# A conformer and attention trunk in fp32: pairs of FF columns moved between two forms of the up-projection

## The chip, the core and the metric

The kernel runs on one core of one Trainium2 chip. A core has engines that run side by side: TensorE (PE; its weight loads are listed as PEld), VectorE (DVE), ScalarE (ACT), GpSimd (POOL) and SyncE (SP), which here only issues DMAs. The metric is device microseconds of one execution; lower is better. The kernel before has a median of 1044.91 us over three runs (1043.2 to 1046.06).

## The reference

512 tokens of width 1024 go through two layers, each followed by a SwiGLU FFN of 2816 columns; a final RMSNorm ends it.

```python
# layer 0: causal conformer convolution, then FFN
h = h + conformer_conv(rmsnorm(h, norm_mix[0]), ...)   # pw1, GLU, 31-tap depthwise conv, LayerNorm, silu, pw2
h = h + swiglu_ffn(rmsnorm(h, norm_ffn[0]), w_up[0], w_down[0])
# one shared k and v, then layer 1: sliding-window attention with sinks, then FFN
kv = rmsnorm(h, norm_kv) @ w_kv
q = rmsnorm(h, norm_mix[1]) @ w_q[0]
h = h + banded_sink_attention(q, k, v, sinks, rel_bias) @ w_o[0]
h = h + swiglu_ffn(rmsnorm(h, norm_ffn[1]), w_up[1], w_down[1])

def swiglu_ffn(x, w_up, w_down):
    gate, up = jnp.split(x @ w_up, 2, axis=-1)
    return (jax.nn.silu(gate) * up) @ w_down
```

All of it is float32.

## The kernel before

Channels lie on partitions, tokens along the free dimension. An fp32 product is made of three matmuls of a reduced type: high by high, high by low and low by high part (`mm3`). Every weight chunk therefore has to be split: `split_weights` casts the high part on ACT (L294) and subtracts the low part on DVE (L297).

Weights come as 258 chunks of 512 KB in an order written out by hand, `PLAN`. `advance` keeps three queues ahead of PE: SP loads nine chunks ahead into six `raw` buffers, ACT and DVE split three ahead into four `whi` and four `wlo` buffers, PE uses. Instructions of an engine run in the order in which the program issues them, so a cast that waits for a buffer holds up what stands behind it. The chunks up to pair 0 of part 0 are not split (`NATIVE`).

An FFN is worked in 11 pairs: pair p has 256 gate and 256 up columns, 4 up chunks and, later, 2 down chunks. There are three forms of the up-projection.

- By token halves (layer 0): part 0 does the first 256 tokens, part 1 the other 256. `HALVES0` gives the pairs, before 0 to 3. Part 1 uses the twin form, in which one matmul of 512 columns and one of 256 do the work of three of 256 (`mm2`, L412 and L413).
- Plain (`plain_pair`): all 512 tokens, matmuls of 512 columns. Before, only layer 1's pair 0.
- By seven products (`SevenPair`, `product`): the block product of 2 x 2 blocks by seven multiplications instead of eight (`SEVEN`), each with 24 matmuls of 256 columns. Sums S1 to S4 of weight blocks are made ahead by accumulating DMAs on POOL's queue (`prepare`, at a pace `share`) and copies on SP's; sums T1 to T4 of the rows in `Rows0.sums` (layer 0, DVE) and `Rows.sums` (layer 1, POOL at L759). A11, A12, ... name the products by their left factor; `take` gathers a product's bank into the four results c11 to c22. Before, layer 0's pairs 4 to 10 and layer 1's pairs 1 to 10.

Layer 0 runs so: the first convolution half, then part 0 (`pw2` of the first half, `ffn_part`), and beside part 0's matmuls the second half's convolution (`Half.background`: taps on DVE, ACT and POOL). `job` gives a background generator points (chunk, step), and `pace` steps it at each chunk. At its end the statistics are turned (`scales_a`, L1067 on PE), spread over the partitions by one matmul (`spread`, L1089), and the rows z are normalised, put through silu and split (`rows`: L1101, L1102, L1103, L544, L545). The products A12 of pairs 4, 5 and 6 that need only first-half rows come early, between part 0 and part 1 (`FIRST`), and ACT copies them (L1257). Part 1 starts with `pw2(h1.z, n1)`, which needs z. Then follow the products of pairs 4 to 10 with `gates` at the end of each pair, their downs, shared k and v, q and attention, o, and layer 1's FFN (`STEPS1`). Layer 1's down projections are by seven too (`low_pairs`).

Of the kernel before, what the change touches and what calls it, by code (L numbers as in the profile page):

```python
# [18 lines left out]
P = 128  # L19
# [38 lines left out]
SEVENS = tuple(range(1, FT // 2))  # L58

def by_seven(layer, pair):  # L60
    return pair in SEVENS if layer else pair >= HALVES0[1][0]


def ups(layer, pair):
    return [("up", layer, pair, half, which) for half in range(2) for which in range(2)]
# [26 lines left out]
def chunk_plan():  # L92
# [12 lines left out]
    for part in range(2):  # L105
        pw2()
        for pair in range(*HALVES0[0]):
            plan.extend(ups(0, pair))
# [15 lines left out]
    for kind, pair in STEPS1:  # L124
        plan.extend(blocks_of(kind, pair) if kind == "low" or by_seven(1, pair) else ups(1, pair))
# [84 lines left out]
def hybrid_trunk(ctx: ExitStack, tc: tile.TileContext, xT, W, prm_in, wdw_in, sinks, relb, onehot, fin, lead, out):  # L210
# [164 lines left out]

    def mm3(out, w, x, start, stop, **kw):
        if w[1] is None:
            nc.tensor.matmul(out, w[0], x, start=start, stop=stop)  # L378
            return
        nc.tensor.matmul(out, w[0], x[0], start=start, stop=False, **kw)  # L380
        nc.tensor.matmul(out, w[0], x[1], start=False, stop=False, **kw)  # L381
        nc.tensor.matmul(out, w[1], x[0], start=False, stop=stop, **kw)  # L382
# [201 lines left out]

    def ffn_part(layer, part, xg, tok, rms, on_h=None, twin=False, plain=None):
# [3 lines left out]
        for g in range(2):  # L589
# [27 lines left out]
            if w == 256:  # L617
                rs_bc = rms.step2().unsqueeze(1).to_broadcast([P, 2, w])
                for e, b in enumerate(full):
                    i = g * 4 + 2 * e  # L620
                    nc.vector.tensor_mul(b, b, rs_bc)
                    nc.vector.tensor_add(hT[:, i:i + 2, tok], b, hT[:, i:i + 2, tok])
                    for k in range(2 if on_h is not None else 0):
                        on_h(i + k)
# [110 lines left out]
    class Rows:  # L735
# [13 lines left out]
        def sums(self):  # L749
# [7 lines left out]
            for name, t, f, a, b in (("T1", t1, nc.gpsimd.tensor_sub, b11, b12), ("T2", b11, nc.gpsimd.tensor_add, b22, t1),  # L757
                                     ("T3", b12, nc.gpsimd.tensor_sub, b22, b12), ("T4", b21, nc.gpsimd.tensor_sub, b11, b21)):
                pool_op(f(t, a, b))  # L759
# [3 lines left out]
                split([both[:, e] for e in range(2)], t, name == "T2")  # L763

# [3 lines left out]
    def plain_pair(pair, rows, pool):  # L768

        banks = accs(512)  # L770
        steps = None
        for half in range(2):
            for which in range(2):
                w = get("up", 1, pair, half, which)
                order = [(k, m) for k in range(4) for m in range(2)]
                if half == 1:
                    order = [(k, m) for m in range(2) for k in range(4)]
                for k, m in order:
                    mm3(banks[which * 2 + m], [a[:, k, m * P:(m + 1) * P] for a in w], rows.x[half * 4 + k],
                        half == 0 and k == 0, half == 1 and k == 3)  # L780
                if half == 0 and which == 0:
                    rows.rms.step1()
                    continue

                if pair == 0:
                    steps = steps or rows.sums()
                    for _ in range(1 + half):
                        next(steps, None)
        rs_bc = rows.rms.step2().rearrange("p (s q) -> p s q", s=2)
        c = new_gates(pool)  # L790
        for m in range(2):
            t = temp()
            nc.vector.tensor_mul(t.rearrange("p (s q) -> p s q", s=2), banks[m].rearrange("p (s q) -> p s q", s=2), rs_bc)
            nc.scalar.activation(t, t, AF.Silu)
            nc.vector.tensor_mul(c[:, m, :, 0, :], banks[2 + m].rearrange("p (s q) -> p s q", s=2),
                                 t.rearrange("p (s q) -> p s q", s=2))
        return c
# [14 lines left out]
    class SevenPair:  # L812

        def __init__(self, kind, pair, rows, c, c11=None):
            self.kind, self.pair, self.rows, self.c, self.early = kind, pair, rows, c, c11
            self.chains = {}

        def take(self, a):
            c11, c12, c21, c22 = (self.c[:, m, s] for m in range(2) for s in range(2))
            chain = CHAINS[a][0]  # L820
# [5 lines left out]
            if a == "A11":  # L826
                if self.early is None:
                    nc.scalar.copy(c11, r)
                else:
                    nc.vector.tensor_add(c11, r, self.early)  # L830
            elif a == "S1":
                nc.scalar.mul(c22, r, -1.0)
            elif a == "S2":
# [864 lines left out]
```

## Time and profile before

The profiled execution took 1043.27 us, 1.64 below the median of the three runs; its span is 1041.5 us, and its mean TensorE clock is 0.997 of full speed.

| engine | busy us | share | instructions |
|---|---|---|---|
| PE | 1031.5 | 99% | 6580 |
| PEld | 932.6 | 90% | 6580 |
| DVE | 776.5 | 75% | 1202 |
| ACT | 613.0 | 59% | 1062 |
| POOL | 473.2 | 45% | 569 |

The span, cut at the first matmul of each stage:

| stage | from us | length us | DVE busy us |
|---|---|---|---|
| first half, pw1 of both | 0 | 128.8 | 107.37 |
| part 0: pw2 | 128.8 | 28.9 | 25.46 |
| part 0: four pairs up | 157.7 | 50.9 | 48.53 |
| part 0: downs | 208.6 | 26.1 | 19.43 |
| three early products | 234.7 | 9.1 | 9.07 |
| part 1: pw2 | 243.8 | 23.0 | 18.77 |
| part 1: ups | 266.8 | 45.9 | 37.62 |
| part 1: downs | 312.7 | 22.5 | 22.30 |
| pairs 4 to 10 by seven | 335.2 | 134.4 | 99.08 |
| their downs | 469.6 | 73.6 | 29.54 |
| kv, q, attention, o | 543.2 | 153.6 | 96.88 |
| layer 1, pair 0 (plain) | 696.8 | 23.1 | 19.66 |
| layer 1, pair 1 | 719.9 | 24.0 | 18.29 |
| layer 1, the rest | 743.9 | 279.7 | 213.25 |
| end | 1023.6 | 17.9 | 11.31 |

How to read the rows in the next sections: a timeline row has the start and the duration in us, engine, line, operation, output<-inputs, partitions x elements, and in brackets the idle time before it with what ended it ("x2": two instructions run together). A row of a wait list has engine and line that waited, the releaser, total us, times, longest us. A stage row has from:to, length, then busy us and count of PE, PEld, DVE, ACT and POOL, the granted TensorE clock, the DMA share and GB/s. A group row has line, engine, operation, shapes and count, then busy us and mean ns of one, then idle time before it. The records of matmuls overlap; their rate is read from start to start.

### The profile page before, as it was taken

Reading aid. Unit: us, or ns where it says so; the run is one execution under the profiler, and the core shown is the slowest. Engines: PE = TensorE matmul, PEld = TensorE weight load, DVE = VectorE, ACT = ScalarE, POOL = GpSimd, SP = SyncE. Lnnn points to the kernel's source line nnn. Section 1 sums busy time; section 2 is a strip of 40 time slices with the busy share of each in tenths; the row PEclk is TensorE's granted clock in tenths of the full one; section 3 lists DMA queues with packets and bytes.
Section 4 is the critical chain, followed back from the end, with each engine's and each line's share of the span. In section 5 each row is a group of like instructions: output and inputs, shape, how many; then the busy total and the mean of one; then the engine's idle time right before and its main releaser. Section 6 shows DMA issues by size and latency. Waiting matters only on the chain.

```text
span 1041.5 us, 17709 instructions
## 1 busy us (share of the span) xinstructions
PE 1031.5 (99%) x6580; PEld 932.6 (90%) x6580; DVE 776.5 (75%) x1202; ACT 613.0 (59%) x1062; POOL 473.2 (45%) x569
## 2 busy tenths in 40 slices
PE   9999999999999999999999999999999999999996
PEld 8888889999988999998888877788989999898995
DVE  3999989978789777673536566678686877868777
ACT  3887798847776556552333565466655556554654
POOL 3999999930535233221214255405442334434134
PEclk9999999999999999999999999999999999999998
DMA  9999747999999988999969766955879988877742
GB/s 356 340 315 207 205 126 204 272 256 275 249 239 262 304 220 284 256 301 244 286 209 254 210 183 183 228 154 152 252 230 312 287 264 264 245 233 222 224 150 81
DMA packets 67282, 248.33 MB, mean 238 GB/s; under 512 B 7579, under 2 KB 13884, under 8 KB 66364
## 3 DMA queue, kind: packets, MB, share of 16 engines
q1 hardware_dynamic: 54236, 200.75, 55.9%
q0 software_dynamic: 12672, 46.14, 24.8%
q8 instruction: 51, 0.84, 0.3%
q10 hardware_dynamic: 288, 0.31, 0.1%
q14 instruction: 35, 0.29, 0.1%
HBM read 241.93 MB, written 97.52 MB: 326 GB/s over the span
## 4 chain that ended last, share of the span: by engine, by line
PE 98%; DMA 0%; DVE 0%; issue 0%; POOLq 0%; SPq 0%; POOL 0%; ACT 0%
PE bank L380 20%; PE bank L382 20%; PE bank L381 20%; PE bank L960 10%; PE bank L902 9%; PE bank L412 4%; PE bank L378 4%; PE bank L413 2%; PE bank L1441 1%; PE bank L1483 1%; PE bank L1470 1%; PE bank L1058 1%; PE bank L1607 1%; PE bank L948 1%; DMA both<-in_lead_dram 0%; PE bank L1562 0%
## 5 line engine op out<-in xcount | busy, mean ns | idle before, releaser
L297 DVE TENSOR_TENSOR wlo<-raw,whi 128x1024 fp32r<-128x1024 f32 x246 | 329.7, 1348 | 136.8 <-ACT whi L294 136.5
L294 ACT CAST whi<-raw 128x1024 fp32r<-128x1024 f32 x246 | 257.1, 1049 | 276.6 <-PE bank L381 194.1
L380 PE MATMUL bank<-quad,whi 128*128 128x256 f32 (+1 forms) x976 | 307.4, 317 | 0.0
L381 PE MATMUL bank<-quad,whi 128*128 128x256 f32 (+1 forms) x976 | 306.6, 315 | 0.0
L382 PE MATMUL bank<-quad,wlo 128*128 128x256 f32 (+1 forms) x976 | 305.7, 315 | 0.0
L380 PEld LDWEIGHTS bank<-quad,whi 128*128 128x128 f32 x976 | 185.5, 191 | 12.8 <-issue 1.6
L381 PEld LDWEIGHTS bank<-quad,whi 128*128 128x128 f32 x976 | 186.0, 191 | 11.9 <-issue 0.5
L382 PEld LDWEIGHTS bank<-quad,wlo 128*128 128x128 f32 x976 | 185.6, 191 | 11.8 <-issue 0.4
L853 POOL TENSOR_TENSOR up<-up 128x512 f32<-128x512 f32 x34 | 62.9, 1851 | 283.6 <-ACT up L850 283.6
L1002 POOL TENSOR_TENSOR pr<-pr,pr 128x256 f32<-128x256 f32 x208 | 155.4, 788 | 2.6 <-ACT pr L1001 2.5
L380 PE MATMUL bank<-rows,whi 128*128 128x256 f32 x488 | 138.0, 283 | 0.0
L381 PE MATMUL bank<-rows,whi 128*128 128x256 f32 x488 | 137.8, 282 | 0.0
L382 PE MATMUL bank<-rows,wlo 128*128 128x256 f32 x488 | 137.8, 282 | 0.0
L1009 DVE SCALAR_TENSOR_TENSOR bank<-apad,wdw,bank 128x256 f32<-128x256 f32 x248 | 112.4, 485 | 3.4
L1001 ACT ACTIVATE pr<-apad,wdw 128x256 f32<-128x256 f32 x208 | 98.3, 502 | 14.9 <-POOL pr L1002 13.1
L960 PE MATMUL bank<-quad,w 128*128 128x256 f32 x448 | 98.7, 380 | 0.0
L960 PEld LDWEIGHTS bank<-quad,w 128*128 128x128 f32 x448 | 84.9, 190 | 11.8 <-DVE bank L1009 0.2
L380 PEld LDWEIGHTS bank<-rows,whi 128*128 128x128 f32 x488 | 93.1, 191 | 0.3
L381 PEld LDWEIGHTS bank<-rows,whi 128*128 128x128 f32 x488 | 93.1, 191 | 0.3
L382 PEld LDWEIGHTS bank<-rows,wlo 128*128 128x128 f32 x488 | 93.0, 191 | 0.0
L491 POOL TENSOR_TENSOR tmp<-tmp,tmp 128x256 f32<-128x256 f32 (+1 forms) x28 | 26.8, 957 | 101.4 <-ACT tmp L487 96.2
L412 PE MATMUL bank<-quad,whi 128*128 128x512 f32 x168 | 59.7, 398 | 0.0
(230 smaller groups left out, 1635.9 us busy)
## 6 DMA issues: line engine op xcount, KB each, us to landing
raw<-in_W_dram SPq DMA_DIRECT2D x170, 512.0 KB, 5.7
raw<-sum SPq DMA_DIRECT2D x88, 512.0 KB, 5.4
sum<-in_W_dram SPq DMA_DIRECT2D x52, 512.0 KB, 6.2
sum<-in_W_dram POOLq DMA_DIRECT2D x44, 512.0 KB, 9.6
sum<-sum POOLq DMA_DIRECT2D x44, 512.0 KB, 8.5
sum<-in_W_dram SPq DMA_DIRECT2D x4, 3584.0 KB, 30.4
w<-in_W_dram SPq DMA_DIRECT2D x14, 512.0 KB, 8.6
sum<-in_W_dram SPq DMA_DIRECT2D x4, 1024.0 KB, 30.3
```

Of the source, the lines that this page charges most:

```text
L294: on_act = nc.scalar.copy(hi, src).ins
L297: latest[:] = [on_act, lo_engine[0].tensor_sub(lo, src, f32(hi)).ins]
L380: nc.tensor.matmul(out, w[0], x[0], start=start, stop=False, **kw)
L381: nc.tensor.matmul(out, w[0], x[1], start=False, stop=False, **kw)
L382: nc.tensor.matmul(out, w[1], x[0], start=False, stop=stop, **kw)
L412: nc.tensor.matmul(first[2], first[0], first[1], start=start, stop=False)
L853: pool_op(nc.gpsimd.tensor_mul(gate, gate, c[:, m, :, 1, :]))
L902: nc.tensor.matmul(out, x, w[:, ws], start=first and e == 0 and i == 0, stop=e == 1 and i == 2, skip_group_check=True)
L960: mm = nc.tensor.matmul(self.pb[:, w * W2:(w + 1) * W2], w1_of(ct, w, k), x[k] if x else xg[k][:, tok], start=k == 0, stop=k == KT - 1)
L1001: on_act = nc.scalar.mul(pr, a[:, j:j + W2], tap(j))
L1002: on_pool = pool_op(nc.gpsimd.tensor_add(pr, acc, pr))
L1009: on_dve = nc.vector.scalar_tensor_tensor(yt if i == nd - 1 else c, src, tap(i), c if i else self.shift, op0=ALU.mult, op1=ALU.add)
```

## The change

Layer 0: `HALVES0` becomes pairs 0 to 2 by halves and 3 to 10 by seven, so pair 3 changes its form. The pairs by seven run as two groups, 3 to 6 and 7 to 10 (`GROUPS0`), each followed by its downs. Twelve early products stand at the end of part 0 (A12 of pairs 3 to 10 and A11 of 4 to 7) where three were; `SevenPair` takes them from buffers (`early`, `p1`). Part 0's updates of h are held and let go two at once and two at the first early products (`let_go`). The convolution job of the second half is spread over 50 paces, and `product` paces once in its middle. The rate of weight sums (`share`) is raised, and one pool has four buffers for five.

Layer 1: `plain_pair` is gone. Pairs 0 and 1 go together by seven (`TWO`): A11, A12 and S4 of both first, which need no T sum, then S1, S2, S3 and A22 of pair 0 and of pair 1; the S4 products have a chain of their own ("w"). The T sums of `Rows.sums` are made on DVE, one step at a time.

```diff
@@ -32,10 +32,14 @@
...
-HALVES0 = ((0, 4), (4, 11))
-FIRST = (4, 5, 6)
+HALVES0 = ((0, 3), (3, 11))
+GROUPS0 = ((3, 7), (7, 11))
+FIRST11 = (4, 5, 6, 7)
+FIRST = [(4, "A11"), (3, "A12"), (4, "A12"), (5, "A11"), (8, "A12"), (5, "A12"),
+         (6, "A11"), (9, "A12"), (6, "A12"), (7, "A11"), (10, "A12"), (7, "A12")]
 LAST = FT // 2 - 1
-STEPS1 = [("up", 0), ("up", 1), ("up", 2), ("low", 0)]
+STEPS1 = [("two", 0), ("up", 2), ("low", 0)]
+TWO = [(p, a) for a in ("A11", "A12", "S4") for p in range(2)] + [(p, a) for p in range(2) for a in ("S1", "S2", "S3", "A22")]
@@ -72,15 +71,14 @@
     return [(kind, pair, n.split()[0]) for n in SEVEN]
 
 
-def part2_products():
+def part2_products(group):
 
     steps, held = [], []
-    for pair in range(*HALVES0[1]):
+    for pair in range(*group):
         names = [n.split()[0] for n in SEVEN]
-        if pair in FIRST:
-            names = ["A11", "S1", "S2", "S4", "S3", "A22"]
+        names = ["A11", "S1", "S2", "S4", "S3", "A22"][pair in FIRST11:]
         steps += [(pair, names[0])] + held
-        held = [(pair, names.pop())] if pair in FIRST else []
+        held = [(pair, names.pop())]
@@ -105,12 +103,13 @@
...
         if part == 0:
-            plan.extend(("up0", pair, "A12") for pair in FIRST)
-    plan.extend(("up0", *step) for step in part2_products())
-    downs(*HALVES0[1])
+            plan.extend(("up0", *step) for step in FIRST)
+    for group in GROUPS0:
+        plan.extend(("up0", *step) for step in part2_products(group))
+        downs(*group)
@@ -122,7 +121,7 @@
...
-        plan.extend(blocks_of(kind, pair) if kind == "low" or by_seven(1, pair) else ups(1, pair))
+        plan.extend([("up", *step) for step in TWO] if kind == "two" else blocks_of(kind, pair))
@@ -582,6 +583,13 @@
...
+    held = []
+
+    def let_go():
+        b, rs_bc, into = held.pop(0)
+        nc.vector.tensor_mul(b, b, rs_bc)
+        nc.vector.tensor_add(into, b, into)
@@ -754,54 +759,28 @@
...
-            for name, t, f, a, b in (("T1", t1, nc.gpsimd.tensor_sub, b11, b12), ("T2", b11, nc.gpsimd.tensor_add, b22, t1),
-                                     ("T3", b12, nc.gpsimd.tensor_sub, b22, b12), ("T4", b21, nc.gpsimd.tensor_sub, b11, b21)):
-                pool_op(f(t, a, b))
+            yield
+            for name, t, f, a, b in (("T1", t1, nc.vector.tensor_sub, b11, b12), ("T2", b11, nc.vector.tensor_add, b22, t1),
+                                     ("T3", b12, nc.vector.tensor_sub, b22, b12), ("T4", b21, nc.vector.tensor_sub, b11, b21)):
+                with tc.issue_after(latest[1]):
+                    f(t, a, b)
...
-    def product(key, block, r, opens, closes=True):
+    def product(key, block, r, opens, between=None):
 
         w = [x.rearrange("p (a k c) -> p a k c", a=2, k=4) for x in get_seven(*key)]
         for which in range(2):
+            if which and between is not None:
+                between()
@@ -811,33 +790,47 @@
...
+            chain = "w" if self.apart and a == "S4" else CHAINS[a][0]
...
+            elif a == "S1" and self.p1 is not None:
+                nc.scalar.copy(c11, self.early["A12"])
+                nc.vector.scalar_tensor_tensor(c22, r, -1.0, self.p1, op0=ALU.mult, op1=ALU.subtract)
@@ -1240,21 +1238,33 @@
...
-        job(second, (base, 0), (base + 8, 19), (base + 13, 22), (base + 26, 40), (base + 30, 45), (base + 34, 50), (base + 35, h1.n_steps - early - 3))
+        job(second, (base, 0), (base + 8, 17), (base + 13, 20), (base + 26, 34), (base + 38, 40), (base + 41, 43), (base + 42, 44),
+            (base + 43, 44), (base + 44, 45), (base + 45, 46), (base + 47, 48), (base + 48, 49), (base + 50, h1.n_steps - early))
...
-        preparing[0], share[0] = prepare(), 0.45
+        preparing[0], share[0] = prepare(), 0.5
...
+        for _ in range(2):
+            let_go()
...
+        chains = {}
+        for n, (pair, a) in enumerate(FIRST):
             pace()
-            r = new_chain()
-            product(("up0", pair, "A12"), [[x0["ffn0"][4 + k][e][:, HALF[0]] for k in range(4)] for e in range(2)], r, True)
-            nc.scalar.copy(first[pair], r)
+            if n < 2:
+                let_go()
+            begins = pair not in chains
+            r = chains.setdefault(pair, new_chain() if begins else None)
+            j = 4 * (a == "A12")
+            product(("up0", pair, a), [[x0["ffn0"][j + k][e][:, HALF[0]] for k in range(4)] for e in range(2)], r, begins, pace)
+            nc.scalar.copy(first[pair][a], r)
@@ -1301,65 +1311,73 @@
...
-    job(rows0.sums(), (base + 11, 0), (base + 19, 8), (base + 26, 14), (base + 32, 17))
+    job(rows0.sums(), (base + 10, 0), (base + 14, 8), (base + 17, 10), (base + 20, 12), (base + 23, 14), (base + 27, 17))
...
+    share[0] = 0.45
+    for group in GROUPS0:
+        lo0, hi0 = group
+        last = hi0 == HALVES0[1][1]
+        hid0, open_pairs = [], {}
+        left = [n for n, _ in part2_products(group)]
+        for pair, a in part2_products(group):
...
+            pace()
+            open_pairs[pair].take(a)
+            left.remove(pair)
+            if pair in left:
+                continue
...
@@ -1571,12 +1589,21 @@
...
-        if by_seven(1, pair):
-            c = seven_pair("up", pair, nxt, new_gates(pool7), flip if pair == SEVENS[0] else None)
-        else:
-            c = plain_pair(pair, nxt, pool7)
-        if pair == SEVENS[0]:
-            flip()
+        if kind == "two":
+            two = [SevenPair("up", p, nxt, new_gates(pool7), apart=True) for p in range(2)]
+            steps = nxt.sums()
+            for n, (p, a) in enumerate(TWO):
+                two[p].take(a)
+                if n == 3:
+                    nxt.rms.step1()
+                for _ in range((1, 2)[n in (2, 3, 4, 5)]):
+                    next(steps, None)
+                if n >= 6:
+                    flip()
+                if a == "A22":
+                    forms[p] = forms_of(two[p].gates(), pool7, p % 2)
+            continue
+        c = seven_pair("up", pair, nxt, new_gates(pool7))
```

On PE, around the spread of the second half's statistics. Here bank_2448 belongs to the last down of part 0, bank_2611 to the first early product; before:

```order
L380 MATMUL bank_2448<-quad_1708,whi_2485 128x256
L381 MATMUL bank_2448<-quad_1709,whi_2485 128x256
L382 MATMUL bank_2448<-quad_1708,wlo_2486 128x256
L1089 MATMUL bank_2601<-tmp_2535,ones_m 128x512
L380 MATMUL bank_2611<-quad_1395,whi_2529 128x256
L381 MATMUL bank_2611<-quad_1395,whi_2529 128x256
```

After, where bank_2742 is that of the eleventh early product, A12 of pair 10:

```order
L381 MATMUL bank_2742<-quad_1398,whi_2657 128x256
L382 MATMUL bank_2742<-quad_1398,whi_2657 128x256
L383 MATMUL bank_2742<-quad_1398,wlo_2658 128x256
L1084 MATMUL bank_2761<-tmp_2702,ones_m 128x512
L381 MATMUL bank_2742<-quad_1398,whi_2657 128x256
L382 MATMUL bank_2742<-quad_1398,whi_2657 128x256
```

The spread stood between a down chunk and the first of three early products, with 72 matmuls of 256 columns behind it until pw2; now it stands in the eleventh of twelve, with 9 matmuls of it and the 24 of the twelfth behind.

On ACT at the same place, from the scaling that the spread reads (L1085, after: L1080) to the second pair of silu steps of z (L1103, after: L1098); CAST whi is a weight chunk, COPY an early product's bank. Before:

```order
L1085 ACTIVATE tmp_2535<-ident,rr_2533 128x128 x2
L294 CAST whi_2615<-raw_2383 128x1024
L294 CAST whi_2653<-raw_2413 128x1024
L294 CAST whi_2710<-raw_2449 128x1024
L1103 ACTIVATE tmp_2605<-tmp_2605,prm 128x256
L1103 ACTIVATE tmp_2644<-tmp_2644,prm 128x256
L544 CAST quad_2603<-tmp_2605 128x256
L544 CAST quad_2603<-tmp_2644 128x256
L1257 COPY quad_2600<-bank_2611 128x512
L294 CAST whi_2760<-raw_2483 128x1024
L1257 COPY quad_2600<-bank_2650 128x512
L1103 ACTIVATE tmp_2682<-tmp_2682,prm 128x256
```

After:

```order
L1080 ACTIVATE tmp_2702<-ident,rr_2700 128x128 x2
L293 CAST whi_2811<-raw_2556 128x1024
L1267 COPY quad_2349<-bank_2707 128x512
L293 CAST whi_2867<-raw_2588 128x1024
L1267 COPY c_2353<-bank_2742 128x512
L1098 ACTIVATE tmp_2765<-tmp_2765,prm 128x256
L1098 ACTIVATE tmp_2784<-tmp_2784,prm 128x256
L545 CAST quad_2763<-tmp_2765 128x256
L545 CAST quad_2763<-tmp_2784 128x256
L293 CAST whi_2898<-raw_2620 128x1024
L1267 COPY c_2350<-bank_2707 128x512
L1098 ACTIVATE tmp_2790<-tmp_2790,prm 128x256
```

Three casts of weights stood between the scaling and the first silu; now two casts and two copies do. Between the second and the third silu stood, beside the casts of z, a weight cast and two copies; now it is a weight cast and one copy.

At the start of layer 1's FFN, on POOL, the T sums (L759) between the DMA issues of the weight sums (L289) and the first statistics (L507), before:

```order
L289 DMA sum_6808<-in_W_dram 128x1024
L759 TENSOR_TENSOR t_7441<-quad_7431 128x1024
L289 DMA sum_6958<-sum_6331 128x1024
L759 TENSOR_TENSOR quad_7431<-quad_7432,t_7441 128x4x256
L759 TENSOR_TENSOR quad_7431<-quad_7432,quad_7431 128x4x256
L759 TENSOR_TENSOR quad_7432<-quad_7431,quad_7432 128x4x256
L507 TENSOR_TENSOR rs_7397<-ms_7395,mhalf 128x4
```

After, they stand on DVE (L766) between the splits of weights (L296), the h rows' splits and squares (L538, L492), the gathering of products (L825) and the splits of T1 (L546):

```order
L492 TENSOR_TENSOR tmp_7379<-tmp_7373,tmp_7379 128x512
L766 TENSOR_TENSOR t_7426<-quad_7416 128x1024
L296 TENSOR_TENSOR wlo_7464<-raw_7199,whi_7463 128x1024
L766 TENSOR_TENSOR quad_7416<-quad_7417,t_7426 128x4x256
L825 TENSOR_TENSOR up_7382<-bank_7460,up_7382 128x512
L296 TENSOR_TENSOR wlo_7503<-raw_7232,whi_7502 128x1024
L766 TENSOR_TENSOR quad_7416<-quad_7417,quad_7416 128x4x256
L825 TENSOR_TENSOR up_7383<-bank_7496,up_7383 128x512
L506 TENSOR_SCALAR ms_7536<-bank_7531 128x4
L546 TENSOR_TENSOR rows_7492<-t_7426,rows_7492 128x1024
L296 TENSOR_TENSOR wlo_7550<-raw_7292,whi_7549 128x1024
L766 TENSOR_TENSOR quad_7417<-quad_7416,quad_7417 128x4x256
```

The four sums moved from POOL to DVE, each with a split of weights behind it.

More of the change, by code (lines that the diff above doesn't have):

```diff
@@ L57, with ups @@
 SEVEN = ("A11 B11", "S1 T1", "S2 T2", "A12 B21", "S3 T3", "S4 B22", "A22 T4")
[L58 to L65, printed above, removed]
+def ups(pair):
+    return [("up", 0, pair, half, which) for half in range(2) for which in range(2)]
 SUMS = {"S1": ("A21", "A22"), "S2": ("A11", "S1"), "S3": ("A21", "A11"), "S4": ("A12", "S2")}
@@ L381, in mm3 @@
         nc.tensor.matmul(out, w[0], x[1], start=False, stop=False, **kw)
-        nc.tensor.matmul(out, w[1], x[0], start=False, stop=stop, **kw)
+        stamp[0] = nc.tensor.matmul(out, w[1], x[0], start=False, stop=stop, **kw).ins
     class Act:
@@ L619, in ffn_part @@
                 for e, b in enumerate(full):
[L620 to L624, printed above, removed]
+                    into = hT[:, g * 4 + 2 * e:g * 4 + 2 * e + 2, tok]
+                    held.append((b, rs_bc, into))
                 continue
```

141 lines of the change are left out of this document (65 added, 76 removed).

## The prediction

> **What bounds the kernel now.** I read the page first: its engine shares and its chain that ended last.
>
> ```profile
> PE 1031.5 (99%) x6580; PEld 932.6 (90%) x6580; DVE 776.5 (75%) x1202; ACT 613.0 (59%) x1062; POOL 473.2 (45%) x569
> PE 98%; DMA 0%; DVE 0%; issue 0%; POOLq 0%; SPq 0%; POOL 0%; ACT 0%
> ```
>
> TensorE (PE) is busy for 99% of the span and 98% of the last chain is its own work. A busy share says little where matmuls are pipelined, so next come the waits of PE, which are the whole list:
>
> ```profile
> PE bank L465 <- POOL ones_m L462: 1.1, 1, 1.1
> PE bank L948 <- DVE quad L922: 0.7, 2, 0.4
> ```
>
> After its start PE waits for nobody. So what counts is how many matmuls of which width PE issues, at what spacing, and whether the change makes PE wait anywhere. The spacing is read from PE's timeline, first and last row of three stretches: 256 columns, 512 columns, and the twin form (one matmul of 512 and one of 256).
>
> ```profile
> 199.73 0.28 PE L382 MATMUL bank<-quad,wlo 128*128 128x256 f32 x1
> ...
> 203.93 0.28 PE L381 MATMUL bank<-quad,whi 128*128 128x256 f32 x1
> ...
> 499.67 0.39 PE L380 MATMUL bank<-quad,whi 128*128 128x512 f32 x1
> ...
> 502.84 0.39 PE L382 MATMUL bank<-quad,wlo 128*128 128x512 f32 x1
> ...
> 300.01 0.39 PE L412 MATMUL bank<-quad,whi 128*128 128x512 f32 x1
> ...
> 302.82 0.40 PE L412 MATMUL bank<-quad,whi 128*128 128x512 f32 x1
> ```
>
> From 199.73 to 203.93 there are 35 steps: 4.20/35 = 0.120 us each. From 499.67 to 502.84 there are 14: 0.2264 us. From 300.01 to 302.82 there are 8 twin pairs: 0.352 us. A weight chunk of 24 matmuls of 256 thus takes 24 x 0.120 = 2.88 us, one of 24 matmuls of 512 takes 5.44, one of 8 twin pairs 2.82.
>
> **The change, part by part. Layer 0, pair 3.** It leaves the token halves: 4 up and 2 down chunks go from part 0 (6 x 2.88 = 17.28 us) and the same from part 1 as twins (6 x 2.82 = 16.92), together 34.20. It comes back as 7 products of 24 matmuls of 256 (7 x 2.88 = 20.16) and 2 down chunks of 512 columns (10.88), together 31.04. That is -3.16 us. The stage rows bear the twin price out:
>
> ```profile
> 266.80:312.70 45.90, 45.90 (x265) 40.03 (x264) 37.62 (x43) 33.23 (x58) 18.94 (x18) 1.00 0.96 258
> 312.70:335.20 22.50, 22.50 (x129) 19.59 (x128) 22.30 (x28) 14.13 (x21) 10.18 (x10) 1.00 0.93 270
> ```
>
> 16 up chunks in 45.90 us and 8 down chunks in 22.50 are 2.87 and 2.81 each.
>
> **Layer 1, pair 0.** Four chunks of 512 (21.76) become seven products (20.16): -1.60 us. Transposes and statistics stay. Sum of both: **-4.76 us** of PE work.
>
> A rule weighed here: the Trainium skill (TensorE: Matmul & The Clock Gate, Back-to-back issue gap) gives a sustained spacing of about 81 ns for 128 columns and 131 ns for 512; between them some 98 ns for 256 is my estimate. The change adds 144 matmuls of 256 and takes away 96 of 512, so by these figures it would add 14.1 - 12.6 = 1.5 us instead of saving time. The trace's 120 and 226 ns decide against it: here two of 256 cost 6% more than one of 512, so seven products against eight save 7% and not 12%, but they save.
>
> **Moved, not removed.** Nine more products stand at the end of part 0 (12, not 3), 9 x 2.88 = 25.9 us of PE work against the 17.28 taken out; they come out of the later product stage, so the sum is unchanged. The remaining convolution steps of the second half run beside part 0, which is now 8.6 us longer. This costs nothing as long as PE has product work there, which it has.
>
> More sums of weight blocks are wanted: two more pairs by seven, so 8 more accumulate transfers on POOL's queue beside these,
>
> ```profile
> sum<-in_W_dram POOLq DMA_DIRECT2D x44, 512.0 KB, 9.6
> sum<-sum POOLq DMA_DIRECT2D x44, 512.0 KB, 8.5
> ACT whi L294 <- PE bank L381: 194.1, 103, 4.4
> ```
>
> and 8 more copies of 512 KB on SP's. The third row (waits of ScalarE, ACT) is why I cost them at nothing: the casts of the weights wait for PE to free a buffer, 194 us in all, so the weights lie there early. The cover is nine chunks of look-ahead, some 26 us of PE time, against a landing in 9.6.
>
> **The wait added: the second half's pw2.** Before it, the normalised rows z must be made: PE spreads the statistics (L1089; L1084 after), then DVE subtracts and multiplies, ACT applies silu and casts, DVE subtracts the low part, row by row.
>
> ```profile
> 234.28 1.02 PE L1089 MATMUL bank<-tmp,ones_m 128*128 128x512 f32 x2
> ...
> 238.08 1.05 ACT L294 CAST whi<-raw 128x1024 fp32r<-128x1024 f32 x1 [2.63 <-PE bank L381]
> 239.04 1.09 ACT L1103 ACTIVATE tmp<-tmp,prm 128x256 f32<-128x256 f32 x2
> 240.03 0.70 ACT L544 CAST quad<-tmp 128x256 fp32r<-128x256 f32 x2
> 240.64 0.57 ACT L1257 COPY quad<-bank 128x512 f32<-128x512 f32 x1
> ...
> 244.12 0.42 DVE L545 TENSOR_TENSOR quad<-tmp,quad 128x256 fp32r<-128x256 f32 x1
> ...
> 251.83 0.75 DVE L545 TENSOR_TENSOR quad<-tmp,quad 128x256 fp32r<-128x256 f32 x2
> ```
>
> The spread ends at 235.30. The three early products follow, so pw2 starts 8.5 us after it, which this stage row shows (PE without a gap):
>
> ```profile
> 234.70:243.80 9.10, 9.10 (x75) 8.85 (x74) 9.07 (x19) 6.46 (x12) 0.00 (x0) 1.00 1.05 270
> ```
>
> After the change the spread stands inside a product: 9 + 24 matmuls, 3.96 us, remain until pw2. I follow ACT from the spread's end (0). A weight cast in line ahead of z waits for the running product's end (9 x 0.120 = 1.08) and ends at 2.13; the copy of a product 2.6; two silus 3.6; the casts of z0 and z1 by 4.3, z0's high part at 4.0 and its low part (0.42 on DVE) at 4.4. PE wants them at 3.96 and a matmul later: about 0.4 late. Then on ACT a weight cast, a copy, three silus and two casts: z2 and z3 stand at about 7.7 to 8.0, low part 8.1, where PE, already 0.4 late, wants z2 at 3.96 + 0.4 + 2.88 = 7.24: 0.8 late. z4 (9.7) is wanted at 10.9: in time. Sum: **+1.2 us**. Lower end 0: the old trace has no such wait. Upper end: from spread to the last low part the old trace took 252.58 - 235.30 = 17.3 us, where PE would now want z7 at 3.96 + 8.64 + 1.56 = 14.2: 3.1 us. I take 1.2 because the old elapsed time holds waits of ACT for PE (2.63 in the row) that shrink when PE is nearer. Behind a waiting PE stand the weight buffers, so ACT's casts and the loads slip along and catch up; nobody else waits.
>
> **Layer 1's start.** Six direct products now come before the first T product. The T sums go from POOL to DVE:
>
> ```profile
> 705.96 8.07 DVE L297 TENSOR_TENSOR wlo<-raw,whi 128x1024 fp32r<-128x1024 f32 x1 [3.44 <-ACT whi L294]
> ...
> 713.96 1.21 DVE L545 TENSOR_TENSOR rows<-t,rows 128x1024 fp32r<-128x1024 f32 x1
> ...
> 702.66 2.41 POOL L759 TENSOR_TENSOR t<-quad 128x1024 f32<-128x1024 f32 x1 [34.98 <-ACT quad L753]
> 705.57 2.67 POOL L759 TENSOR_TENSOR quad<-quad,t 128x1024 f32<-128x1024 f32 x1
> 707.93 5.01 POOL L759 TENSOR_TENSOR quad<-quad,quad 128x1024 f32<-128x1024 f32 x2
> ```
>
> POOL's four sums took 10.1 us, and one weight split that ran beside them took 8.07 us where the row after it, as wide, takes 1.21. On DVE I price four sums by that row, 4 x 1.21 = 4.8, and 6.9 us of stretched split go. The stage of both pairs, with DVE third in the row of busy times:
>
> ```profile
> 696.80:743.90 47.10, 47.10 (x308) 42.80 (x306) 37.95 (x37) 32.46 (x45) 19.92 (x14) 1.00 0.62 178
> ```
>
> DVE becomes 37.95 - 6.9 + 4.8 = 35.9 of 47.1 - 1.6 = 45.5 us. PE did not wait here before, so what is freed earns nothing, and the six products (17.3 us) cover the four sums. I take 0; ends 0 and +1.2, one sum standing in the way of a split.
>
> **Sum**: 1043.27 (the profiled execution: span 1041.5 and 1.8 around it) - 4.76 + 1.2 = 1039.7. The median of the three runs, 1044.91, is 1.64 above that execution, so the time I give is 1044.91 - 4.76 + 1.2 = **1041.3 us**, -0.34%. 0.3% (3.1 us, about what a measurement of this kernel can tell from no change) lies at 1041.8 and 1048.0, so the forecast is near the border.
>
> **Rivals.** (1) The waits eat the gain: z late by the full 3.1, or 1 to 2 us more at the layer 1 start or between the two groups, whose last gate must be done before its downs. For: PE has no slack to lose them in. Against: no late engine in the old rows. 1044.91 - 4.76 + 3.1 = 1043.3, to 1045.
>
> (2) The other side: VectorE becomes the bound in group 1, the products of pairs 3 to 6.
>
> ```profile
> 335.20:469.60 134.40, 134.40 (x1106) 133.40 (x1105) 99.08 (x114) 74.57 (x98) 39.28 (x29) 1.00 0.92 272
> L297 DVE TENSOR_TENSOR wlo<-raw,whi 128x1024 fp32r<-128x1024 f32 x46 | 60.0, 1309 | 22.6 <-ACT whi L294 22.5
> L849 DVE TENSOR_TENSOR up<-up,rsbc 128x512 f32<-128x512 f32 x13 | 8.9, 686 | 0.1
> ```
>
> The old stage has DVE at 99 of 134 us. In group 1 seven of 28 products were taken out beforehand, but the gates stay: 21 products, 60.5 us of PE, against 21 splits x 1.31 = 27.5 and some 42 operations of 512 columns (6 per pair of gates and low parts, 18 bank additions) x 0.69 = 29.0, together 56.5, or 93%. To end slower by 3.1, PE must lose 4.76 + 3.1 = 7.9 us, so DVE must need 68.4: every operation 21% longer. For: the 8.07 us split shows what stretching is possible, and splits here already average 1.31 against the 1.21 above. Against: POOL, beside which that happened, is busy in only 39 of these 134 us. It would give 1048 to 1050.
>
> (3) PE is paced by its weight loads, so 48 more matmuls cost 48 loads.
>
> ```profile
> L380 PEld LDWEIGHTS bank<-quad,whi 128*128 128x128 f32 x976 | 185.5, 191 | 12.8 <-issue 1.6
> ```
>
> 48 x 0.191 = +9.2: 1054. Against: matmuls of 256 start every 0.120 us, below the 0.191 of a load's record, and those of 512 twice as far apart though they load as often. This is the case in which the skill's spacing above, counted per matmul, would also hold; by its figures 1046.4.
>
> (4) The change does not do what it says: not seven for eight. The order of instructions excludes it: 144 more of 256 and 96 fewer of 512 on PE.
>
> **How the numbers follow.** Forecast (waits up to about 2 us) 0.62; rival 1 0.20; rival 2 0.14; rival 3 0.02; 0.02 for anything else, on the slow side. The forecast's cases spread over the border of 1041.8 with most below; rival 1 lies between the borders. Faster 0.58, same 0.25, slower 0.17. Range: low end is no wait at all (1040.2) less the 1.7 by which the lowest old run lies under its median, 1038.4; high end takes in rival 1 and the edge of rival 2, 1047.5.
>
> **What would show it.** Right: PE's waits grow by about a microsecond, at the first matmul of the second pw2 and two chunks of it, waiting for z; up and down stages of part 1 17 us shorter; no 8 us split at layer 1's start; PE with about 48 more matmuls and a span some 3.5 us shorter. Wrong: PE waits for DVE in the products of pairs 3 to 6, whose DVE share is above 95%; a wait at the boundary of the groups; the spacing of 256-column matmuls above 0.120 us there; or PE idle for weights in the sum blocks.

## The result: slower by 0.46%

The changed kernel has a median of 1049.1 us (five runs, 1048.78 to 1051.16) against 1044.91 for the kernel before (now five runs, 1043.2 to 1046.06): a ratio of 1.0046, 95% interval 1.0034 to 1.0057. This ratio is that of the two means; the medians alone give 1.0040. The forecast was 1041.3 us, a ratio of 0.9965. The page of the changed kernel, engine shares and the chain that ended last:

```profile
PE 1032.6 (99%) x6628; PEld 934.4 (89%) x6628; DVE 795.7 (76%) x1226; ACT 612.0 (58%) x1062; POOL 474.9 (45%) x575
PE 92%; DVE 4%; issue 1%; DMA 1%; ACT 0%; POOL 0%; POOLq 0%; SPq 0%; DVEq 0%; ACTq 0%
```

PE still has 99%, but its part of the last chain fell from 98% to 92%, and VectorE has 4% of it. The waits of PE, the longest first:

```profile
PE bank L381 <- DVE up L808: 2.8, 1, 2.8
...
PE bank L383 <- DVE wlo L296: 0.9, 1, 0.9
PE bank L414 <- DVE wlo L296: 0.8, 2, 0.6
PE bank L382 <- DVE quad L546: 0.6, 2, 0.4
```

One wait stands out. It is at the start of group 1: A11 of pair 3 is done, S1 goes into another bank, and S2 needs A11's bank again, which VectorE has to read out first (L808). PE's and VectorE's timelines there:

```profile
337.43 0.28 PE L383 MATMUL bank<-rows,wlo 128*128 128x256 f32 x1
340.47 0.36 PE L381 MATMUL bank<-rows,whi 128*128 128x256 f32 x1 [2.76 <-DVE up L808]
...
342.82 0.41 PE L381 MATMUL bank<-rows,whi 128*128 128x256 f32 x1
343.03 0.41 PE L382 MATMUL bank<-rows,whi 128*128 128x256 f32 x1
...
335.84 1.40 DVE L613 TENSOR_TENSOR tmp<-bank,tmp 128x256 f32<-128x256 f32 x4
337.17 1.69 DVE L296 TENSOR_TENSOR wlo<-raw,whi 128x1024 fp32r<-128x1024 f32 x1
338.78 0.94 DVE L615 TENSOR_TENSOR h<-h,tmp 128x256 f32<-128x256 f32 x1
339.64 0.68 DVE L808 TENSOR_TENSOR up<-bank,quad 128x512 f32<-128x512 f32 x1
```

PE stops for 3.04 us start to start, 2.92 more than a step. And then the matmuls stand 0.21 us apart instead of 0.12, 17 of them, 1.55 us in all. The stage rows say why VectorE is late and why the matmuls are slow (the clock is the third number from the end):

```profile
313.60:331.80 18.20, 17.38 (x97) 14.52 (x96) 18.00 (x22) 12.20 (x21) 7.07 (x6) 1.00 1.03 306
340.40:345.00 4.60, 4.53 (x26) 4.56 (x27) 3.19 (x5) 0.23 (x1) 2.38 (x3) 0.64 1.03 309
```

In part 1's downs VectorE is busy for 18.00 of 18.20 us; it enters group 1 with a backlog. It was as full before, 22.30 of 22.50 us. But over the ups and downs of part 1 together its work fell from 59.92 to 46.64 us, by 13.3, and PE's matmuls by 16.9. After the wait the granted clock is 0.64 in the mean of 4.6 us, 0.50 in the middle of it.

Stage by stage, from the first matmul of each (profiled executions, 1041.5 and 1047.9 us of span):

| stage | matmuls alone, us | measured change, us | lost, us |
|---|---|---|---|
| up to part 0 (the same in both) | 0 | +0.7 | 0.7 |
| part 0 with early products | +8.6 | +10.3 | 1.6 |
| part 1: pw2 | 0 | +1.3 | 1.3 |
| part 1: ups and downs | -16.9 | -15.6 | 1.3 |
| pairs 3 to 10 and their downs | +5.1 | +9.6 | 4.5 |
| kv, q, attention, o | 0 | 0 | 0 |
| layer 1's FFN | -1.6 | +0.2 | 1.8 |

The matmuls alone sum to -4.8, the losses to 11.2, together the 6.4 us by which the spans differ. The medians differ by only 4.2: the profiled execution of the old kernel lies 1.64 us below its median, that of the changed one 0.62 above, so some 2 us of the losses belong to these two executions. The first row's start moves by up to 1.8 us between the profiled executions of the kernels below (by 0.8 among those with the old layer 0).

### The profile page after: what moved, and what is told of

It is laid out like the page before. It is cut to its first block, busy times and chain, and to the rows that moved or that the text cites. A ratio compares the mean times of both kernels' runs of the same rounds, so it can differ in the third digit from the quotient of the medians.

```text
span 1047.9 us, 17857 instructions
## 1 busy us (share of the span) xinstructions
PE 1032.6 (99%) x6628; PEld 934.4 (89%) x6628; DVE 795.7 (76%) x1226; ACT 612.0 (58%) x1062; POOL 474.9 (45%) x575
## 4 chain that ended last, share of the span: by engine, by line
PE 92%; DVE 4%; issue 1%; DMA 1%; ACT 0%; POOL 0%; POOLq 0%; SPq 0%; DVEq 0%; ACTq 0%
PE bank L381 20%; PE bank L383 20%; PE bank L382 20%; PE bank L955 10%; PE bank L895 9%; PE bank L379 4%; DVE wlo L296 2%; PE bank L413 2%; PE bank L1459 1%; PE bank L1501 1%; PE bank L1488 1%; PE bank L414 1%; PE bank L1053 1%; PE bank L1634 1%; DMA both<-in_lead_dram 1%
## 5 line engine op out<-in xcount | busy, mean ns | idle before, releaser
L296 DVE TENSOR_TENSOR wlo<-raw,whi 128x1024 fp32r<-128x1024 f32 x246 | 323.5, 1323 | 115.9 <-ACT whi L293 111.2
L382 PE MATMUL bank<-quad,whi 128*128 128x256 f32 (+1 forms) x968 | 302.7, 313 | 0.6 <-DVE quad L546 0.6
L381 PE MATMUL bank<-quad,whi 128*128 128x256 f32 (+1 forms) x968 | 302.5, 315 | 0.3 <-ACT quad L1267 0.2
L383 PE MATMUL bank<-quad,wlo 128*128 128x256 f32 (+1 forms) x968 | 301.5, 313 | 0.9 <-DVE wlo L296 0.9
L846 POOL TENSOR_TENSOR up<-up 128x512 f32<-128x512 f32 x38 | 72.2, 1900 | 324.1 <-ACT up L843 297.6
L381 PE MATMUL bank<-rows,whi 128*128 128x256 f32 x544 | 154.6, 285 | 2.9 <-DVE up L808 2.8
L382 PE MATMUL bank<-rows,whi 128*128 128x256 f32 x544 | 154.3, 284 | 0.0
L383 PE MATMUL bank<-rows,wlo 128*128 128x256 f32 x544 | 154.0, 284 | 0.0
L381 PEld LDWEIGHTS bank<-rows,whi 128*128 128x128 f32 x544 | 104.3, 192 | 3.9 <-issue 3.2
L382 PEld LDWEIGHTS bank<-rows,whi 128*128 128x128 f32 x544 | 104.5, 192 | 0.5 <-issue 0.2
L383 PEld LDWEIGHTS bank<-rows,wlo 128*128 128x128 f32 x544 | 104.3, 192 | 0.0
L492 POOL TENSOR_TENSOR tmp<-tmp,tmp 128x256 f32<-128x256 f32 (+1 forms) x28 | 26.9, 961 | 64.3 <-ACT tmp L488 59.5
L895 PE MATMUL bank<-wlo,fhi 128*128 128x512 f32 x140 | 55.3, 395 | 0.0
```

The source lines that it names most:

```text
L296: latest[:] = [on_act, lo_engine[0].tensor_sub(lo, src, f32(hi)).ins]
L383: stamp[0] = nc.tensor.matmul(out, w[1], x[0], start=False, stop=stop, **kw).ins
L846: pool_op(nc.gpsimd.tensor_mul(gate, gate, c[:, m, :, 1, :]))
L895: nc.tensor.matmul(out, x, w[:, ws], start=first and e == 0 and i == 0, stop=e == 1 and i == 2, skip_group_check=True)
```

## The experiments

Each run has its own runs of the kernel before beside it, so ratios are compared, the changed kernel's being 1.0046. Intervals are about 1 us to either side of a ratio, and some 1.5 us for the difference of two.

**Each layer alone.** `l0_only` is the changed kernel with layer 1's old FFN, `l1_only` the old kernel with layer 1's new one.

```diff
# l0_only, against the changed kernel
-STEPS1 = [("two", 0), ("up", 2), ("low", 0)]
+STEPS1 = [("up", 0), ("up", 1), ("up", 2), ("low", 0)]
# and plain_pair, the old Rows.sums and the old loop over STEPS1; l1_only is the reverse, made on the kernel before
```

> The changed kernel with layer 1's FFN as it was before: pair 0 plain, the T sums on POOL, seven products in the old order; layer 0 stays changed. In the two traces the changed kernel reaches layer 1's FFN 6.2 us later than the old one (702.99 against 696.75 us) and takes 344.9 us from there against 344.8. Theory A (layer 0 alone loses, by a wait of PE for VectorE at the start of group 1 and the slow matmuls after it, and layer 1's gain of 1.6 us is lost to its own small waits): 1051 us, the same wait of about 2.9 us at the second product of pair 3. Rival B (the extra weight sums and their transfers slow everything a little, wherever they are): about 1047, with half of the loss.

> The kernel before with only layer 1's change: pairs 0 and 1 together by seven, six direct products first, T sums on VectorE. By matmuls alone 1.6 us less. Theory A: 1043.5 to 1045, the gain mostly lost to waits of PE of under 1 us each at pair 0's last two products and in the down block of pairs 0 and 1. Rival B (sums and transfers): 1046 to 1047. If the pair order itself is sound and the waits in the changed kernel came from layer 0's shift in time: 1043.3.

Measured: `l0_only` 1048.61 us, 1.0045 (1.003 to 1.006); `l1_only` 1044.91 us, 1.0009 (1.000 to 1.0018). Layer 0 carries the whole loss, with the same wait of 2.8 us at the gather. Layer 1's new order, worth 1.6 us of matmuls, ends 0.9 us above zero: in its trace stand a delay of 0.4 us in the products, where PE waits for a bank that VectorE reads out, and one of 1.1 in the down block of pairs 0 and 1, the same as in the changed kernel. The second has a weight split of 4.30 us beside POOL's additions (VectorE's and POOL's timelines of the changed kernel):

```profile
782.76 4.30 DVE L296 TENSOR_TENSOR wlo<-raw,whi 128x1024 fp32r<-128x1024 f32 x1
...
783.18 2.79 POOL L902 TENSOR_TENSOR h<-h,tmp 128x512 f32<-128x512 f32 x2
```

The rival that the extra weight sums slow everything predicted half of the loss in each; it falls.

**The gather taken off VectorE.**

```diff
-                if "A12" in self.early:
+                if "A12" in self.early and self.pair != HALVES0[1][0]:
                     nc.vector.tensor_add(c11, r, self.early["A12"])
                 else:
                     nc.scalar.copy(c11, r)
...
                 nc.vector.tensor_sub(c22, c22, r)
+                if "A12" in self.early and self.pair == HALVES0[1][0]:
+                    nc.vector.tensor_add(c11, c11, self.early["A12"])
```

> The changed kernel with one change: the bank of pair 3's first product A11 is copied out by ScalarE, and VectorE adds the early product to it later, in the order after S3. So the next product into that bank no longer stands behind VectorE's queue. Theory A (VectorE's late gather costs 2.9 us of waiting and 1.5 us of half-speed matmuls after it): 4.4 us less, 1044.7 us, and no stretch of matmuls at 0.21 us. Rival C (VectorE is behind by 3 us anyway and the wait only moves to the next product, which needs a low weight part or the second gather): less than 1.5 us gained, a wait on VectorE of 2 us or more right behind.

Measured: 1045.62 us, 1.0019 (1.001 to 1.0029), 2.8 us less than the changed kernel by the ratios. ScalarE's and VectorE's rows:

```profile
336.10 0.59 ACT L810 COPY up<-bank 128x512 f32<-128x512 f32 x1
...
341.39 0.68 DVE L829 TENSOR_TENSOR up<-up,quad 128x512 f32<-128x512 f32 x1
```

ScalarE empties the bank at 336.1, in time; VectorE adds at 341.4, with nobody waiting. The wait and the slow matmuls are gone. 0.7 us of it comes back two products later as a wait for a weight split, because VectorE is as far behind as before. So the gather's place in VectorE's queue cost some 3.5 us (2.8 and the 0.7), the clock included.

**The spread earlier.** The job's points behind (base + 26, 34) were moved four paces forward:

```diff
-(base + 38, 40), (base + 41, 43), (base + 42, 44), (base + 43, 44), ..., (base + 48, 49), (base + 50, h1.n_steps - early)
+(base + 34, 40), (base + 37, 43), (base + 38, 44), (base + 39, 44), ..., (base + 44, 49), (base + 46, h1.n_steps - early)
```

> The changed kernel with the last steps of the second half's convolution job (statistics, spread, z rows) due four paces, two early products, earlier. Theory: the second pw2 then waits as little as before, 24.3 us become 23.1, so 1.2 us less: 1047.9. Rival: the waits there come from ScalarE's order of casts, copies and silus, whatever the spread's place, and the statistics' own waits move into the early products: within 0.4 us of 1049.1.

Measured: 1047.38 us, 1.0031 (1.0019 to 1.0042), 1.6 us less by the ratios. In the changed kernel PE had waited within the second chunk of pw2 for z; here no wait stands in that stage, which takes 23.1 us where it took 24.3. In the changed kernel the spread's input was ready some 2 us before the spread ran, so the job's points, not the work, had made it late.

**The T sums later.** Two versions of the job's points: `tsums_later` moves T3 and T4 into group 1, `t4_later` T4 alone.

```diff
-job(rows0.sums(), ..., (base + 20, 12), (base + 23, 14), (base + 27, 17))
+job(rows0.sums(), ..., (base + 20, 12), (base + 28, 12), (base + 29, 13), (base + 30, 14), (base + 31, 15), (base + 32, 18))  # tsums_later
+job(rows0.sums(), ..., (base + 20, 12), (base + 23, 14), (base + 30, 14), (base + 31, 15), (base + 32, 18))  # t4_later
```

> The changed kernel with one change: the job that makes layer 0's T sums does T3 and T4 (two sums and two splits, 4.9 us of VectorE by the rows L1305 and L546) beside the first products of pair 3 and not in part 1's last five downs. Theory A (VectorE is full in part 1's downs, 18.00 of 18.20 us, because one pair fewer stands there and the T sums are the same): the gather of A11 comes some 4 us earlier, the 2.9 us wait and the slow matmuls go, and so do the two waits of 0.7 and 0.4 us in the downs: 5 to 5.5 us less, 1043 to 1044. Rival C (the gather of A11 is what is too slow, or the weight split ahead of it): the wait stays above 2 us, 1048.

Measured: 1047.04 us, 1.0021 (1.0011 to 1.0031). The two waits in the downs went, but the wait at the gather stayed at 2.8 us: a miss. VectorE's timeline there:

```profile
335.94 1.75 DVE L1305 TENSOR_TENSOR plain<-plain 128x1024 f32<-128x1024 f32 x1
337.61 0.75 DVE L615 TENSOR_TENSOR h<-h,tmp 128x256 f32<-128x256 f32 x2
338.28 0.68 DVE L808 TENSOR_TENSOR up<-bank,quad 128x512 f32<-128x512 f32 x1
```

The moved sum of T3 (L1305) landed right ahead of the gather, and PE, no longer held up in the downs, came 1.4 us earlier to wait for it. That left open whether the backlog or a fixed chain behind the last banks delays the gather; T4 alone was to tell.

> The changed kernel with T4 alone moved out of part 1's downs (one sum and one split, 2.5 us of VectorE), to where PE runs pair 3's later products; T3 stays. With T3 moved too, the sum landed right ahead of the gather of A11 and the wait stayed. Theory A (VectorE's backlog at the end of the downs is what delays the gather): the waits of 0.7 and 0.4 us in the downs go, the wait at the gather falls from 2.9 to 0.5 to 1.5 us, and below about 1.3 us no slow matmuls follow: 3 to 4.5 us less than the changed kernel, a ratio of 1.0005 to 1.002 to the kernel before. Rival C (the gather is late by a fixed chain behind the downs' last banks, whatever VectorE still has to do): the wait stays at 2.8 us, ratio 1.0035 to 1.0045.

Measured: 1046.41 us, 1.0013 (1.0004 to 1.0022), 3.4 us less by the ratios. The gather starts at 337.85 instead of 339.64, and PE waits 1.25 us more than a step, now for a weight cast of ScalarE's that ended 0.06 us behind the gather, with no slow matmul behind. So the gather's lateness is a backlog and no fixed chain: 2.5 us taken out of VectorE's queue bring it 1.8 us forward. The waits of 0.7 and 0.4 us in the downs stay here, against the expectation; they go only where T3 is moved too.

**Idle work in the old kernel.**

```diff
+idle = temp(); nc.vector.memset(idle, 0.0)
+for _ in range(n): nc.vector.tensor_add(idle, idle, idle)   # n = 5, n = 2
 nc.vector.tensor_add(c11, r, self.early)                    # pair 4's A11
```

> The kernel before with nothing but idle work: VectorE gets a fill and five additions of 512 columns on a spare tile, about 3.3 us, right ahead of the gather of pair 4's A11. In the old trace that gather ended 0.3 us before PE wanted the bank. Theory A: PE waits 2.9 us there, then runs some 17 matmuls at 0.213 us, and the kernel is 4.4 us slower. Rival D (the slow matmuls in the changed kernel came from something else at that place, such as a transfer): a wait of 2.9 us and matmuls at 0.12 us right after.

> As the run with five additions, but two, about 1.5 us: PE waits about 1.2 us. If the slow stretch follows any wait over a microsecond, 1.5 us more is lost; if it needs a longer one, only the 1.2 us are lost, as after the waits of 0.7 us in the changed kernel, behind which no slow matmul is seen.

Measured: 1046.24 and 1045.72 us, one run each, beside 1044.98. The experiment was less than planned: of five additions the program's order put only two ahead of the gather, so both are the same delay. PE's timeline with five:

```profile
342.67 0.28 PE L382 MATMUL bank<-rows,wlo 128*128 128x256 f32 x1
343.80 0.36 PE L380 MATMUL bank<-rows,whi 128*128 128x256 f32 x1 [0.86 <-DVE up L835]
343.99 0.28 PE L381 MATMUL bank<-rows,whi 128*128 128x256 f32 x1
344.11 0.27 PE L382 MATMUL bank<-rows,wlo 128*128 128x256 f32 x1
```

Even so VectorE's lateness alone makes the old kernel wait at this place, and after a gap of 1.1 us the matmuls run at 0.12 us at once. The wait of 2.9 us that was to be made did not arise, so what a long wait does to the old kernel's matmuls at this place was not tried. Nor do the two times give the price of the delay: both traces also hold a wait of 1.0 us at 200 us, ahead of the edit, for a weight split that took 4.36 us beside POOL.

**Layer 0's three changes together, with the old layer 1.** `best2` takes T3 and T4 later, `best3` T4 alone; `best4` is `best3` with the new layer 1.

> All three changes to layer 0 together (A11's bank copied by ScalarE, statistics and spread four paces earlier, T3 and T4 later), and layer 1's FFN as it was before. If theory A has named the main losses of layer 0, what is left of them is under 1.5 us, and the 3.16 us of matmuls saved there show: 0.997 to 0.9985 of the kernel before, about 1041.5 to 1042.5 us. If further losses hide behind those removed: 1.000 or above.

Measured: 1043.13 us, 0.9985 (0.9976 to 0.9994). In PE's timeline, ScalarE's, and the stage row after it:

```profile
337.03 0.28 PE L383 MATMUL bank<-rows,wlo 128*128 128x256 f32 x1
338.78 0.39 PE L381 MATMUL bank<-rows,whi 128*128 128x256 f32 x1 [1.48 <-ACT whi L293]
...
336.74 1.05 ACT L545 CAST rows<-plain 128x1024 fp32r<-128x1024 f32 x1 [3.63 <-DVE plain L1335]
337.69 1.04 ACT L293 CAST whi<-raw 128x1024 fp32r<-128x1024 f32 x1
...
339.50:343.10 3.60, 3.60 (x19) 3.60 (x19) 3.60 (x4) 1.95 (x4) 0.00 (x0) 0.53 1.07 273
```

ScalarE stood 3.63 us for T3's sum, and the weight cast behind it came too late; the gap of 1.75 us was followed by slow matmuls again. This profiled execution was the slowest of the ten (1045.28 us), and the median lies at the upper edge of the range expected.

> Layer 1's FFN as before, and in layer 0 A11's bank copied by ScalarE, statistics and spread four paces earlier, and T4 alone later. In the version with T3 later too, ScalarE's cast of T3 held up the weight casts behind it: PE waited 1.6 us and ran 1.5 us slower. If that was the last large loss: 2.5 to 3 us below that version, ratio 0.9965 to 0.9975 to the kernel before. If the layer 0 change carries another loss of that size elsewhere: 0.998 to 0.999.

> As the version with T4 later and the old layer 1, but with layer 1 changed as in the changed kernel. If layer 1's change loses by its own waits (three of 0.3 to 1.1 us against 1.6 us of matmuls saved), the ratio is 0.0005 to 0.001 higher than that version's. If its loss in the changed kernel came from layer 0's shift: 0.0015 lower.

Measured: `best3` 1042.86 us, 0.9978 (0.9968 to 0.9988); `best4` 1043.46 us, 0.9984 (0.9975 to 0.9994). `best3` beats both kernels. Its whole list of waits of PE:

```profile
PE bank L466 <- POOL ones_m L463: 1.1, 1, 1.1
PE bank L414 <- DVE wlo L296: 0.8, 2, 0.6
PE bank L973 <- DVE quad L945: 0.5, 2, 0.3
PE bank L382 <- DVE quad L546: 0.4, 1, 0.4
```

What is left in layer 0 is mainly the pair of waits for weight splits in part 1's downs, where T3's sum and split still stand, and one of 0.4 us in part 0. The gain of 2.3 us by the ratio, of 3.16 in matmuls, fits. It lies just above the range expected. `best4`'s 0.0006 more lies within the intervals; it agrees with `l1_only`, and does not show by itself that layer 1's order loses.

**The T sums of layer 1 on POOL.**

```diff
-("T1", t1, nc.vector.tensor_sub, b11, b12), ...   # on the old kernel with the new layer 1
+("T1", t1, nc.gpsimd.tensor_sub, b11, b12), ...
```

> The kernel before with layer 1's change, but with the four T sums left on POOL. Prediction's claim: on VectorE they are worth nothing either way. If VectorE's 4.8 us for the sums are what makes PE wait at pair 0's S2 and S3 (0.8 and 0.3 us): those two waits go, about 1 us less than with the sums on VectorE. If POOL's sums stretch the weight splits beside them, as the 8.07 us split in the kernel before: T rows and splits come later, 1 to 3 us more.

Measured: 1050.7 us, 1.0052 (1.0038 to 1.0066), 4.5 us more than with the sums on VectorE. The waits of PE, VectorE's timeline and the stage row behind the wait:

```profile
PE bank L383 <- DVE wlo L298: 5.5, 2, 4.4
...
707.96 8.00 DVE L298 TENSOR_TENSOR wlo<-raw,whi 128x1024 fp32r<-128x1024 f32 x1 [3.44 <-ACT whi L295]
...
716.00:719.60 3.60, 3.59 (x17) 3.60 (x18) 3.60 (x6) 0.00 (x0) 1.16 (x1) 0.50 0.93 155
```

The 8 us split of the old kernel is there again, beside POOL's sums; PE, which now reaches that chunk earlier, waits 4.4 us for it and then runs at half clock for 3.6 us. The list's other wait, 1.0 us, stands at 200 us in part 0, where the code is the old kernel's; so of the 4.5 us about 1 may not be the sums' doing.

## Why the prediction was wrong

- **The matmul counts and spacings** held: 0.12 us per matmul of 256 except behind long waits, and `best3` keeps most of layer 0's 3.16 us. Rival 3 fell: with 48 more loads the spacing stayed the same.
- **"The wait added: the second half's pw2", 1.2 us**, was right in place and size: the stage is 1.3 us longer, and with an earlier spread 1.2 of it come back in the trace (1.6 us by the ratios). The first of the two waits, 0.4 us at z0, did not occur; the second, at z2, did with 0.7.
- **The step that failed is "Layer 0, pair 3"**. It priced the pair's leaving of part 1 as PE time alone. That pair was also 17 us of cover for VectorE, which makes the T sums there whatever the number of pairs: VectorE lost 13.3 us of work, 3.6 less than PE did. The row quoted in that step had VectorE at 22.30 of 22.50 us in the downs, and was read only for the twin price. The old trace had 0.3 us of margin at the place:

```profile
339.93 0.68 DVE L830 TENSOR_TENSOR up<-bank,quad 128x512 f32<-128x512 f32 x1
...
340.93 0.28 PE L380 MATMUL bank<-rows,whi 128*128 128x256 f32 x1
```

  The gather ended at 340.61 and PE wanted the bank at 340.93. After the change it is 2.9 us late, and part 1's ups and downs lose 1.3 us more. `t4_later`, which shortens VectorE's queue, and `a11_on_act`, which takes the read-out off it, show that this queue is the cause; `best3` does both, and its list has no wait at this place.
- **The sum had no term for the clock.** A wait was priced at its length. Here 2.9 us cost 4.5, with the 1.55 us of slow matmuls.
- **Rival 2 named the engine and not the mechanism.** VectorE's 56.5 of 60.5 us over all of group 1 did not decide; over 21 products it was no bound, and PE does not wait for it once it has caught up. A backlog carried into the first three products did. And 7.9 us need not be lost in one place: 4.5 were, the rest in several.
- **"Layer 1's start: I take 0; ends 0 and +1.2"**: 1.8 us were lost in layer 1's FFN, more than the gain of 1.6: 0.7 in pairs 0 and 1, within those ends, and 1.1 in their down block, which was in no term. That freeing VectorE of the stretched split "earns nothing" was right against the old order and wrong for the new one, where the sums on POOL would cost 4.5 us, or about 3.5 without the wait in part 0.
- Part 0's 1.6 us and the 0.7 at the start were in no term. Of part 0's, 0.5 is a delay at 204 us and 0.4 a wait for ScalarE's copy of an early product at 232 us; for the rest of it no run was made, and its cause stays open.

## What to carry to other kernels

When a change takes work from the busiest engine, look up what other engines do beside that work: where a stage row has the second engine at 99%, as here, what is cut from the first engine alone becomes a backlog of the second, and the first instruction behind the stage which PE needs from that engine pays for it. Put the read-out of a bank that is wanted again on the engine with the shorter queue, and give a job's due points anew when the stage they count through is shortened. Price a wait of PE above some 1.5 us with the slow matmuls that can follow it, here 1.4 to 1.8 us.

## What the runs showed of the hardware

- In all traces the granted clock changes at whole multiples of 3.41 us, counted from its first record. In the changed kernel's step with the long wait PE is busy for 1.22 of 3.41 us, at full clock; the next step is at half clock:

```profile
338.28:341.69 3.41, 1.22 (x10) 1.25 (x11) 3.41 (x5) 0.94 (x2) 3.41 (x5) 1.00 1.05 253
341.69:345.10 3.41, 3.41 (x18) 3.41 (x17) 1.90 (x4) 0.33 (x1) 1.09 (x2) 0.50 1.03 333
```

- Away from the kernel's start and end, a step at clock 0.5 followed each step in which PE stood still for 1.37 us or more (1.37, 1.48, 1.86, 2.19, 2.33, 2.79 and 3.08 us, in six traces), and none followed a step with 1.09 us or less (1.09 in `t4_later`, 1.02 and 0.86 in `delay5`). Nothing lies between. At 0.5, matmuls of 256 columns stood 0.213 us apart for 0.120. So a gap counts by what falls of it into one step, and one of 1.75 us, as in `best2`, might at another place in the steps be followed by nothing; no run shows that. The slow matmuls began up to 1.55 us after PE's restart (`spread_earlier`); in `l1_pool_sums` the half clock came within the gap of 4.72 us and lasted two steps. The Trainium skill (TensorE: Matmul & The Clock Gate, HAM oscillation) tells of a fall to half clock after idle gaps of more than about 3.4 us; here a gap of 1.75 us was enough, so the measurement decides. Its half speed and its window of about 3.4 us agree with the clock of 0.50 and the steps of 3.41 us.
- A weight split of 1.21 us on VectorE took 8.00 and 4.30 us beside POOL operations of 1024 and 512 columns. The T sums of layer 1, moved to VectorE, took 1.22 us each, and so did the splits between them. Which engine is stretched can change: at about 200 us, in code that the two kernels share, two splits took 1.61 and 1.47 us while POOL's six additions took 6.49 (the kernel before), and one split took 4.36 while they took 4.45 (`delay5`).
